# Two-layer encoder trunk: later load of x's second half, weight-sum transfers that wait, ordered splits, and a first 1/rms by GpSimd

## The chip, the cores and the metric

The kernel runs on one core of a Trainium2 chip. The metric is the device time of one execution in microseconds. Its engines are named as the profile names them: PE (TensorE, matrix products), DVE (VectorE), ACT (ScalarE), POOL (GpSimd) and SP (SyncE, which here only issues transfers). Each engine runs its own list of instructions in order; an instruction waits until those it depends on, on other engines or in transfers, are done, and holds up everything behind it in its list.

## The reference, cut to what matters

Two request groups (512 and 256 tokens, 768 in all, 1024 wide) go through two layers with shared weights, in float32. A layer is a half feed-forward, a mixer and a half feed-forward; the mixers don't matter here.

```python
def rmsnorm(x, g):
    y = x32 * lax.rsqrt(jnp.mean(x32 * x32, axis=-1, keepdims=True) + EPS)
    return y.astype(x.dtype) * g

def swiglu(h, wg, wu, wd):              # D_MODEL 1024, D_FF 2816
    return (jax.nn.silu(h @ wg) * (h @ wu)) @ wd

def even_layer(x, ...):                 # odd_layer: another mixer
    x = x + 0.5 * swiglu(rmsnorm(x, f1_n), f1_g, f1_u, f1_d)
    x = x + mixer_ab(rmsnorm(x, mix_n), ...)
    x = x + 0.5 * swiglu(rmsnorm(x, f2_n), f2_g, f2_u, f2_d)
    return x
```

## The kernel before, in words

Six phases follow one another: a feed-forward, a mixer, two feed-forwards (the second half of layer 0 and the first of layer 1), a mixer and a feed-forward. x lies transposed in eight tiles x0 to x7 (128 features by 768 tokens); its tokens are two halves of 384 columns.

Every float32 product is made of three products of rounded parts: high by high, low by high, high by low. A weight tile's high part `whi` is a cast on ACT (line 122), its low part `wlo` a subtraction on DVE (line 123). The operands made from x are split in the same way: `gain_split` (lines 404 to 410, high part on ACT at 407, low on DVE at 408) multiplies by the norm's gain, `split` (208, 209) has no gain.

A feed-forward goes through 11 pairs of weight columns, each for gate and for up. For a pair, seven products by sums of quarters replace eight (Strassen's scheme as Winograd wrote it). Their moving operands, made from x, are b11, b21, t2, t3, n4, t1 and b22; each consists of four tiles (b110 to b113). The stationary ones are quarters of the weights or sums of them: `s1` is the sum of two quarters, `s2` is `s1` and another quarter, `s3` a sum of quarters too. For most pairs DVE makes s1. For some, the early pairs among them, POOL issues a transfer that loads the first quarter into s1 and then a second that adds the other to it (`added`, line 642): a load and an accumulating load in series, for gate and for up, called weight-sum transfers here. Chain 1 makes the s1 of a feed-forward's first pair, chain 2 that of its second.

In each feed-forward the first four pairs begin early. A pair first runs two products that need neither norm nor sums, `p1` (with b11) and `p2` (with b21). `ORDERS` (line 46) mixes these steps: (0, 1, 0, 1, 2, 2, 0, 1, 3, 2, 3, 3). `p1`'s result in PSUM is copied by ACT (line 603) into a tile `p1`; `self.copied` lists those copies, two to a pair. The fifth is thus the gate's copy of the third pair. `hidden` makes the hidden units (`sg`, `v`: lines 587 to 590), which frees the PSUM banks. Later `settle` runs the other five products of a pair, first t2, which needs s2.

PE's order is as written; on the other engines and for transfers a scheduler orders instructions by priority and estimated times. `issue_after(ins)` tells it to place instructions behind `ins`; it is not a wait at run time on another engine. So before the change, the POOL queue began the first weight-sum transfers at 5.71 us, though they were placed behind a copy.

At the start, loads come on SP in the order written in `build` (from line 1684): x's first half mixed with the first four weight tiles (`first`), then x's second half, six tiles `tok` (x by tokens, for the sums of squares), and raw weight tiles of 512 KB. `second` (line 462) feeds the second half's operands, once `SECOND` copies have been scheduled. `tok_norm` (line 259) squares and sums tok on ACT, and `rsqrt` (line 314) makes 1/rms on DVE by an integer guess and three refinements (lines 317 to 328, twelve instructions on 128x3). `diags` writes it on diagonals, with which PE spreads it over the partitions.

Of the kernel before, what the change touches and what calls it, by code (L numbers as in the profile page):

```python
# [38 lines left out]
DELAYT = (0.0, 14.0), (0.0, 14.0)  # L39
TOKW, TOKQ, SECOND = (2, 8), (0, 6), 2  # L40
STEPS = (2.5, 1.5, 1.5)
# [14 lines left out]
class Trunk:  # L56
# [4 lines left out]
    def __init__(self, ctx, tc, aps, phases=PHASES):  # L61
        self.tc, self.nc, self.aps, self.phases = tc, tc.nc, aps, phases
        self.units = []
        self.woff = self.pi = 0
        self.t = 0.0
        self.chains = []
        self.spare = []
        self.first = []
        self.copied = []
        self.exps = []  # L70
# [12 lines left out]
        self.guards = {}  # L83
        self.side = "left"
# [14 lines left out]
    def raw(self, name, k0, nk, c0, n, raw=None, eng=None, **kw):  # L99
# [5 lines left out]
        if raw is None:  # L105
            raw = self.rawp.tile([P, nk * n], F32, tag="raw", name=f"raw{i}")
        (eng or self.nc.sync).dma_start(raw, src, **kw)  # L107
        if self.spare and i >= 20:
# [27 lines left out]
    def silu(self):  # L136

        self.nc.scalar.activation(self.space, self.ones[:, :96], AF.Silu)

# [119 lines left out]
    def tok_norm(self, h):  # L259
# [12 lines left out]
        with self.tc.high_priority() if h == 0 else nullcontext():  # L272
            nc.vector.tensor_tensor(out=a, in0=a, in1=b, op=ALU.add)
            self.rsqrt(y, a, 1.0 / D, a, b, it[:, :3])
            self.early[h] = self.diags(y)
# [37 lines left out]

    def rsqrt(self, y, src, scale, v, h, it):

        nc = self.nc
        nc.vector.tensor_scalar(out=v, in0=src, scalar1=scale, scalar2=EPS, op0=ALU.mult, op1=ALU.add)
        nc.vector.tensor_scalar(
# [85 lines left out]
    def gain_split(self, n, k, src, m):  # L404

        hi, lo = self.b[n][k]
        self.nc.scalar.activation(hi, src, AF.Copy, scale=self.gain(m))
        self.nc.vector.scalar_tensor_tensor(
            out=lo, in0=src, scalar=self.gain(m), in1=hi.bitcast(F32), op0=ALU.mult, op1=ALU.subtract
        )  # L410

# [50 lines left out]
    def second(self):  # L462

        while len(self.copied) < SECOND:
            yield 0.2
        with self.tc.issue_after(self.copied[SECOND - 1]):
            for m in [i // 2 + (0 if i % 2 else 4) for i in range(KD)]:
                self.feed(m, 1)
# [9 lines left out]
    def ffn(self, pre):  # L478
# [5 lines left out]
        urgent = (0, EARLY - 1) if self.first else (EARLY - 1,)  # L484
        behind = len(self.copied) + (3 if self.first else 5)
        hs = {}
# [40 lines left out]
        def pair(p):  # L527
# [24 lines left out]
            def product(n, w, b, key, start, st=None):  # L552
# [4 lines left out]
                with ExitStack() as stack:  # L557
                    if early and b in ("b11", "b21"):
                        stack.enter_context(self.tc.high_priority())
                    if early and not fresh and b in ("b11", "b21"):  # L560
                        if len(order) >= NW and order[-NW]:
# [35 lines left out]
            def p1():  # L597
                for n in names:
                    product(n, a[n, 1, 1], "b11", "X", True)
                    if early:  # L600
                        e[n, "p1"] = etile("p1")
                        with self.tc.high_priority():
                            self.copied.append(nc.scalar.copy(e[n, "p1"], bank["X", n]).ins)
                            order[-1:] = [self.copied[-1]]
                    else:
# [35 lines left out]

            def added():
                for n in names:
                    t = s[n, "s1"] = self.fw.tile([P, 4, P], F32, tag="s", name="s1", bufs=8)
                    for k, kw in ((4, {}), (0, {"accum_op": ALU.add})):
                        self.raw(f"{pre}_w_{n}", k, 4, (2 * p + 1) * P, P, t.rearrange("p a b -> p (a b)"), nc.gpsimd, **kw)
# [50 lines left out]
            if early:  # L697
                if p + 1 < EARLY - 1:
                    addeds[p + 1]()
                settle(now)  # L700
# [7 lines left out]
        for i, p in enumerate(ORDERS[mixed]):  # L708
            next(stages[p])
            if i == 8:  # L710
                with self.tc.issue_after(self.copied[behind]):
                    addeds[0]()
        for p in range(NPAIR):
# [927 lines left out]
    def build(self):  # L1641
# [17 lines left out]
        nc.gpsimd.memset(self.ones, 1.0)  # L1659
        nc.vector.tensor_copy(self.onesr, self.ones)  # L1660
        self.space = space
        self.silu()
        make_identity(nc, self.ident)
        self.gains = self.cp.tile([P, 64], F32, tag="gains", name="gains")[:, : KD * len(NORMS)]
# [19 lines left out]
        for h, (c0, c1) in enumerate(HALVES):  # L1684
            for m in range(KD):
                nc.sync.dma_start(self.x[m][:, c0:c1], self.aps["x"][m, :, c0:c1])
                if kind == "f":
                    if h == 0:
                        self.feed(m, 0)
                else:  # L1690
# [135 lines left out]
```

## Time and profile before

| | us |
|---|---|
| three runs | 2589.17, 2592.65, 2595.09 (median 2592.65) |
| the profiled execution | 2590.38, of which its span 2588.6 |
| PE busy | 2552.2 (99%) |
| DVE busy | 2232.6 (86%) |
| ACT busy | 1366.6 (53%) |
| POOL busy | 155.5 (6%) |

The mean granted clock of PE is 0.996. The times in a row of the trace are its start, in microseconds from the span's start, and its length; in brackets stand the idle time of that engine before it and what ended it. Names are those of the program without buffer numbers, and a line is often a helper's: line 152 is every product, line 122 every high part of a weight.

### The profile page before, as it was taken

To read this page: it belongs to the slowest core of one execution; us is meant where nothing else is said; L and a number is where in the kernel's file an instruction comes from. 1 tells how busy PE (TensorE), PEld (TensorE's weight loads), DVE (VectorE), ACT (ScalarE), POOL (GpSimd) and SP (SyncE) were. 2 spreads that over 40 slices of the span, in tenths; PEclk is the share of its full clock that TensorE was granted. 3 is DMA by queue.
4 is the path that set the end of the run, shared out by engine and by line. 5 is a ranking of instruction groups with operands and counts; after the bars stand their busy time and mean duration, and the time that the engine had idled before them with its cause. 6 is when DMAs were issued, how large, how long until landed. Compare 5 with 4: busy or idle time off the path is not lost.

```text
span 2588.6 us, 41317 instructions
## 1 busy us (share of the span) xinstructions
PE 2552.2 (99%) x15114; PEld 2487.2 (96%) x15114; DVE 2232.6 (86%) x4662; ACT 1366.6 (53%) x2869; POOL 155.5 (6%) x252
## 2 busy tenths in 40 slices
PE   8999999999999999999999999999999999999998
PEld 8999999988899999999999999998998999999997
DVE  7988898978879989889998889886776699888897
ACT  7544454646656545445654445454455575444543
POOL 1000000000021000000100000001222220000000
PEclk9999999999999999999999999999999999999999
DMA  7523222331144322222542222242221343222222
GB/s 246 170 81 106 72 74 74 124 100 46 58 125 132 114 66 74 74 66 98 136 109 82 66 77 71 66 145 64 64 64 41 106 134 119 82 74 74 71 66 76
DMA packets 93372, 238.68 MB, mean 92 GB/s; under 512 B 21488, under 2 KB 34288, under 8 KB 93168
## 3 DMA queue, kind: packets, MB, share of 16 engines
q1 hardware_dynamic: 85712, 218.96, 26.3%
q0 software_dynamic: 7168, 16.78, 3.1%
q8 instruction: 119, 1.95, 0.3%
q14 instruction: 85, 0.70, 0.1%
q10 hardware_dynamic: 288, 0.29, 0.0%
HBM read 226.56 MB, written 15.07 MB: 93 GB/s over the span
## 4 chain that ended last, share of the span: by engine, by line
PE 89%; DVE 6%; ACT 2%; DMA 1%; issue 1%; SPq 0%; DVEq 0%; ACTq 0%
PE ps_mm L152 54%; PE ps_aux L152 34%; PE ps_aux L156 1%; DVE wlo L123 1%; ACT p L1109 1%; DVE p L1103 1%; DMA raw<-in_w 1%; DVE tl L209 0%; DMA x<-in_x 0%; DVE tmp L415 0%; DVE p L1119 0%; ACT whi L122 0%; DVE s L739 0%; DMA first<-in_w 0%; DVE o L1254 0%
## 5 line engine op out<-in xcount | busy, mean ns | idle before, releaser
L122 ACT CAST whi<-s 128x512 fp32r<-128x512 f32 x496 | 304.6, 620 | 407.3 <-DVE s L739 177.6
L122 ACT CAST whi<-raw 128x512 fp32r<-128x512 f32 x504 | 306.1, 619 | 222.9 <-PE ps_mm L152 91.3
L123 DVE TENSOR_TENSOR wlo<-s,whi 128x512 fp32r<-128x512 f32 x496 | 336.8, 684 | 61.0 <-ACT whi L122 53.4
L123 DVE TENSOR_TENSOR wlo<-raw,whi 128x512 fp32r<-128x512 f32 x471 | 321.7, 691 | 18.2 <-ACT whi L122 14.5
L152 PE MATMUL ps_mm<-db,whi 128*128 128x384 f32 x864 | 219.2, 334 | 0.0
L152 PE MATMUL ps_aux<-dt,whi 128*128 128x384 f32 x864 | 219.2, 334 | 0.0
L152 PEld LDWEIGHTS ps_aux<-dt,whi 128*128 128x128 f32 x864 | 156.0, 188 | 0.0
L152 PEld LDWEIGHTS ps_mm<-db,whi 128*128 128x128 f32 x864 | 156.0, 188 | 0.0
L152 PE MATMUL ps_mm<-xh,whi 128*128 128x512 f32 (+1 forms) x416 | 146.2, 352 | 0.0
L152 PE MATMUL ps_aux<-dt,wlo 128*128 128x384 f32 x432 | 144.4, 334 | 1.4 <-DVE wlo L123 1.4
L152 PE MATMUL ps_mm<-db,wlo 128*128 128x384 f32 x432 | 144.3, 334 | 0.0
L152 PE MATMUL ps_mm<-xh,wlo 128*128 128x512 f32 (+1 forms) x416 | 141.3, 340 | 0.0
L152 PE MATMUL ps_mm<-xl,whi 128*128 128x512 f32 (+1 forms) x416 | 141.2, 339 | 0.0
L739 DVE TENSOR_TENSOR s<-raw,raw 128x512 f32<-128x512 f32 x124 | 84.0, 685 | 25.7 <-DMA raw<-in_w 25.5
L578 DVE TENSOR_TENSOR u<-ps_aux,u 128x384 f32<-128x384 f32 x176 | 96.9, 550 | 4.9 <-PE ps_aux L152 4.8
L152 PE MATMUL ps_aux<-dh,whi 128*128 128x384 f32 x384 | 97.5, 334 | 0.0
L795 DVE TENSOR_TENSOR x<-ps_aux,x 128x384 f32<-128x384 f32 x160 | 85.3, 551 | 14.1 <-PE ps_aux L152 13.8
L1109 ACT ACTIVATE p<-p,st 128x256 f32<-128x256 f32 (+3 forms) x144 | 68.9, 480 | 49.3 <-DVE st L1107 49.2
L573 ACT COPY u<-ps_mm 128x384 f32<-128x384 f32 x176 | 83.5, 475 | 16.5 <-PE ps_mm L152 15.9
L795 DVE TENSOR_TENSOR x<-ps_mm,x 128x384 f32<-128x384 f32 x160 | 86.1, 550 | 7.1 <-PE ps_mm L152 6.8
L107 POOL DMA_DIRECT2D s<-in_w x64 | 47.1, 781 | 702.2 <-PE ps_aux L152 387.6
L152 PEld LDWEIGHTS ps_mm<-xh,whi 128*128 128x128 f32 x416 | 79.8, 192 | 9.3 <-issue 0.9
(516 smaller groups left out, 8134.1 us busy)
## 6 DMA issues: line engine op xcount, KB each, us to landing
raw<-in_w SPq DMA_DIRECT2D x346, 512.0 KB, 3.7
s<-in_w POOLq DMA_DIRECT2D x64, 256.0 KB, 5.0
xdm<-x SPq DMA_DIRECT2D x16, 384.0 KB, 2.4
x<-in_x SPq DMA_DIRECT2D x16, 192.0 KB, 6.3
tok<-in_xt SPq DMA_DIRECT2D x12, 256.0 KB, 6.5
xold<-xdm SPq DMA_DIRECT2D x8, 384.0 KB, 3.1
x<-xdm SPq DMA_DIRECT2D x8, 384.0 KB, 4.7
out_y<-y SPq DMA_DIRECT2D x8, 384.0 KB, 2.4
```

The lines of the kernel that those rows point to most:

```text
L107: (eng or self.nc.sync).dma_start(raw, src, **kw)
L122: nc.scalar.copy(hi, src)
L123: (eng or nc.gpsimd).tensor_tensor(out=lo, in0=src, in1=hi.bitcast(F32), op=ALU.subtract)
L152: self.nc.tensor.matmul(out, lhsT=lhsT, rhs=rhs, start=start, stop=stop, **kw)
L156: self.nc.tensor.transpose(out, src, self.ident)
L573: nc.scalar.copy(e[n, out], bank[key, n])
L578: nc.vector.tensor_tensor(out=t, in0=bank[key, n], in1=t, op=ALU.add)
L739: f = lambda o, x, y, op: self.nc.vector.tensor_tensor(out=o, in0=x, in1=y, op=op)
L795: nc.vector.tensor_tensor(out=o, in0=ps, in1=o, op=ALU.add)
L1103: nc.vector.tensor_tensor_reduce(out=outs[i], in0=ps_list[i], in1=adds[i], scale=1.0, scalar=init[i], op0=ALU.add, op1=ALU.max, accum_out= ...
L1109: ins = nc.scalar.activation(outs[i], outs[i], AF.Exp, bias=nm[:, i : i + 1], accum_out=sm[:, i : i + 1])
```

## The change

Four things change in the program's text.

1. `SECOND` is 6 and no longer 2. x's second half isn't loaded by `build` any more, but by `second`, once six copies have been scheduled, and placed behind the last raw load issued so far (`self.loading`). On SP the eight transfers now stand behind the six tok tiles and the first two raw loads, and ahead of the next two raw loads.
2. `added(then)` has POOL copy one element per partition of the `then`-th p1 copy into s1 ahead of its loads. The loads overwrite it and so wait for it. Chain 1 waits for the fifth copy of its feed-forward, chain 2 for the eighth. All four feed-forwards call it.
3. The first half's b11 splits of x0 to x3 have priority and are placed one behind the other, and the b11 products' weight splits behind the last of them.
4. The first 1/rms is made by one DVE instruction and GpSimd's power to -0.5, by a constant in eight columns of `space` which the warm-up activation no longer writes.

```diff
-TOKW, TOKQ, SECOND = (2, 8), (0, 6), 2
+TOKW, TOKQ, SECOND = (2, 8), (0, 6), 6
...  raw()
-        (eng or self.nc.sync).dma_start(raw, src, **kw)
+        self.loading = (eng or self.nc.sync).dma_start(raw, src, **kw).ins
...  silu()
-        self.nc.scalar.activation(self.space, self.ones[:, :96], AF.Silu)
+        self.nc.scalar.activation(self.space[:, :88], self.ones[:, :88], AF.Silu)
...  tok_norm()
-            self.rsqrt(y, a, 1.0 / D, a, b, it[:, :3])
+            self.rsqrt(y, a, 1.0 / D, a, b, it[:, :3], h == 0)
...  rsqrt(..., power=False)
+        if power:
+            nc.vector.tensor_scalar(out=v, in0=src, scalar1=scale, scalar2=EPS, op0=ALU.mult, op1=ALU.add)
+            nc.gpsimd.tensor_tensor(out=y, in0=v, in1=self.half[:, : v.shape[1]], op=ALU.pow)
+            return
...  gain_split()
-        self.nc.scalar.activation(hi, src, AF.Copy, scale=self.gain(m))
-        self.nc.vector.scalar_tensor_tensor(
+        ins = self.nc.scalar.activation(hi, src, AF.Copy, scale=self.gain(m)).ins
+        self.fed = ins, self.nc.vector.scalar_tensor_tensor(
             out=lo, in0=src, scalar=self.gain(m), in1=hi.bitcast(F32), op0=ALU.mult, op1=ALU.subtract
-        )
+        ).ins
...  second()
+        with self.tc.issue_after(self.loading):
+            for m in range(KD):
+                self.nc.sync.dma_start(self.x[m][:, H:T], self.aps["x"][m, :, H:T])
...  ffn()
-        behind = len(self.copied) + (3 if self.first else 5)
+        behind = len(self.copied) + 4
...  product()
+                    for ins in self.fed4 if fresh and early and b == "b11" and (p or n == "up") else ():
+                        stack.enter_context(self.tc.issue_after(ins))
...  p1()
+                            self.ps1.append(e[n, "p1"])
...
-            def added():
+            def added(then=None):
                 for n in names:
                     t = s[n, "s1"] = self.fw.tile([P, 4, P], F32, tag="s", name="s1", bufs=8)
+                    if then:
+                        nc.gpsimd.tensor_copy(t[:, 0, 0:1], self.ps1[then][:, 0:1])
...
-                    addeds[p + 1]()
+                    addeds[p + 1](behind + 3 if p == 0 else None)
...
             if i == 8:
-                with self.tc.issue_after(self.copied[behind]):
-                    addeds[0]()
+                addeds[0](behind)
...  build()
+        self.half = space[:, 88:96]
+        nc.gpsimd.memset(self.half, -0.5)
...
             for m in range(KD):
-                nc.sync.dma_start(self.x[m][:, c0:c1], self.aps["x"][m, :, c0:c1])
+                if kind != "f" or h == 0:
+                    nc.sync.dma_start(self.x[m][:, c0:c1], self.aps["x"][m, :, c0:c1])
                 if kind == "f":
                     if h == 0:
-                        self.feed(m, 0)
+                        with ExitStack() as stack:
+                            if m < 4:
+                                stack.enter_context(self.tc.high_priority())
+                            for ins in self.fed if 0 < m < 4 else ():
+                                stack.enter_context(self.tc.issue_after(ins))
+                            self.feed(m, 0)
+                            self.fed4 = self.fed if m < 4 else self.fed4
```

The scheduler's estimates change with this, and so does the order on DVE and ACT at places far from the edit. PE's order stays as it was, but for the two products by the second half's diagonals, which stand one product earlier. In the order of the changed kernel the line numbers are larger by 1 at the top of the file and by 12 further down (739 is 751, 587 is 597, 603 is 613, 795 is 807).

DVE in the first feed-forward, before: where the fourth pair's first product gets its bank (`sg` and `v` from the ps_mm banks read the early pairs' first products), and the first user of a weight-sum transfer (s_716, from s_606).

```order
L123 TENSOR_TENSOR wlo_619<-raw_556,whi_618 128x512
L415 SCALAR_TENSOR_TENSOR tmp<-x_104,ngains,tmp 128x384
L209 TENSOR_TENSOR t30l<-tmp,t30h 128x384
L587 TENSOR_TENSOR sg<-ps_mm_252,acc 128x384
L589 TENSOR_TENSOR v<-ps_mm_271,acc 128x384
L587 TENSOR_TENSOR sg<-ps_mm_290,acc 128x384
L123 TENSOR_TENSOR wlo_684<-raw_558,whi_683 128x512
L739 TENSOR_TENSOR s_716<-s_606,raw_708 128x512
L589 TENSOR_TENSOR v<-ps_mm_375,acc 128x384
```

The same place after; s_592 is now the transferred sum.

```order
L751 TENSOR_TENSOR s_705<-s_592,raw_697 128x512
L210 TENSOR_TENSOR t22l<-tmp,t22h 128x384
L420 SCALAR_TENSOR_TENSOR tmp<-tmp,ngains 128x384
L420 SCALAR_TENSOR_TENSOR tmp<-x_104,ngains,tmp 128x384
L597 TENSOR_TENSOR sg<-ps_mm_245,acc 128x384
L124 TENSOR_TENSOR wlo_708<-s_705,whi_707 128x512
L599 TENSOR_TENSOR v<-ps_mm_264,acc 128x384
L597 TENSOR_TENSOR sg<-ps_mm_283,acc 128x384
L599 TENSOR_TENSOR v<-ps_mm_325,acc 128x384
```

The sum s moved from behind `sg`, `v` and `sg` to ahead of them all.

DVE near 150 us, before: the first down projection ends (it adds to the x tiles), and the five products of the fourth pair begin with t2. s_1776 is its gate's s2 and s_1782 its up's; sg, u and db belong to the pair before.

```order
L795 TENSOR_TENSOR x_108<-ps_aux_1536,x_108 128x384
L739 TENSOR_TENSOR s_1776<-s_1462,raw_1764 128x512
L795 TENSOR_TENSOR x_109<-ps_aux_1545,x_109 128x384
L123 TENSOR_TENSOR wlo_1779<-s_1776,whi_1778 128x512
L795 TENSOR_TENSOR x_110<-ps_aux_1554,x_110 128x384
L739 TENSOR_TENSOR s_1776<-raw_1764,s_1776 128x512
L209 TENSOR_TENSOR db_1805<-sg,db_1804 128x384
L497 TENSOR_TENSOR sg<-u_1248,sg 128x384
L739 TENSOR_TENSOR s_1782<-s_1467,raw_1770 128x512
L739 TENSOR_TENSOR s_1808<-raw_1764,raw_1767 128x512
```

After, where the gate's s2 is s_1770 and the up's s_1776:

```order
L807 TENSOR_TENSOR x_108<-ps_aux_1521,x_108 128x384
L807 TENSOR_TENSOR x_109<-ps_aux_1530,x_109 128x384
L807 TENSOR_TENSOR x_110<-ps_aux_1539,x_110 128x384
L751 TENSOR_TENSOR s_1776<-s_1461,raw_1764 128x512
L807 TENSOR_TENSOR x_111<-ps_aux_1548,x_111 128x384
L751 TENSOR_TENSOR s_1802<-raw_1758,raw_1761 128x512
L124 TENSOR_TENSOR wlo_1779<-s_1776,whi_1778 128x512
L751 TENSOR_TENSOR s_1776<-raw_1764,s_1776 128x512
L124 TENSOR_TENSOR wlo_1805<-s_1802,whi_1804 128x512
L210 TENSOR_TENSOR db_1799<-sg,db_1798 128x384
L751 TENSOR_TENSOR s_1825<-raw_1764,raw_1767 128x512
L505 TENSOR_TENSOR sg<-u_1242,sg 128x384
```

The up's s2 moved from behind `db` and `sg` to between the last two additions to x.

DVE near 290 us, where a down projection follows on a pair, before: v reads the pair's last product, s_3268 is a sum of two raw weight tiles for the down projection.

```order
L587 TENSOR_TENSOR sg<-ps_mm_2977,acc 128x384
L739 TENSOR_TENSOR s_3268<-raw_3258,raw_3261 128x512
L589 TENSOR_TENSOR v<-ps_mm_2996,acc 128x384
L739 TENSOR_TENSOR s_3270<-s_3268,raw_3258 128x512
L590 SCALAR_TENSOR_TENSOR sg<-sg,v 128x384
L123 TENSOR_TENSOR wlo_3277<-s_3268,whi_3276 128x512
L123 TENSOR_TENSOR wlo_3313<-raw_3252,whi_3312 128x512
```

After, where it is s_3262:

```order
L597 TENSOR_TENSOR sg<-ps_mm_2971,acc 128x384
L599 TENSOR_TENSOR v<-ps_mm_2990,acc 128x384
L600 SCALAR_TENSOR_TENSOR sg<-sg,v 128x384
L210 TENSOR_TENSOR dt_3351<-sg,dt_3350 128x384
L751 TENSOR_TENSOR s_3262<-raw_3252,raw_3255 128x512
L751 TENSOR_TENSOR s_3264<-s_3262,raw_3252 128x512
L751 TENSOR_TENSOR s_3444<-raw_3246 128x512
L124 TENSOR_TENSOR wlo_3271<-s_3262,whi_3270 128x512
```

It moved from ahead of `v` to behind `v`, `sg` and `dt`.

ACT in the fourth phase (layer 1's first feed-forward), before: s_14398 is s2 of the first pair, made from the transferred sum; the copy p_14292 is the first of the fourth pair, and p2 of that pair, which adds to the same bank ps_mm_14273, waits for it.

```order
L122 CAST whi_14366<-raw_14271 128x512
L588 ACTIVATE sg<-sg 128x384
L122 CAST whi_14400<-s_14398 128x512
L122 CAST whi_14412<-s_14410 128x512
L603 COPY p_14292<-ps_mm_14273 128x384
L595 COPY ps_mm_14416<-p_14006 128x384
L595 COPY ps_mm_14438<-p_14029 128x384
L122 CAST whi_14434<-s_14432 128x512
L603 COPY p_14334<-ps_mm_14294 128x384
```

After, where s2 has the number 14398 too and the copies are p_14290 and p_14332:

```order
L123 CAST whi_14366<-raw_14269 128x512
L123 CAST whi_14400<-s_14398 128x512
L605 COPY ps_mm_14418<-p_14004 128x384
L613 COPY p_14290<-ps_mm_14271 128x384
L605 COPY ps_mm_14440<-p_14027 128x384
L613 COPY p_14332<-ps_mm_14292 128x384
L598 ACTIVATE sg<-sg 128x384
L123 CAST whi_14414<-s_14412 128x512
```

The gate's `whi` stands ahead of that copy in both, the up's moved behind both copies. What s_14398 waits for is new: its weight-sum transfer now follows the fifth copy, p_14196, six rows above.

More of the change, by code (lines that the diff above doesn't have):

```diff
@@ L69, in __init__ @@
         self.copied = []
+        self.ps1 = []
         self.exps = []
@@ L312, in diags, with rsqrt @@
         return res
-    def rsqrt(self, y, src, scale, v, h, it):
+    def rsqrt(self, y, src, scale, v, h, it, power=False):
         nc = self.nc
+        if power:
+            nc.vector.tensor_scalar(out=v, in0=src, scalar1=scale, scalar2=EPS, op0=ALU.mult, op1=ALU.add)
+            nc.gpsimd.tensor_tensor(out=y, in0=v, in1=self.half[:, : v.shape[1]], op=ALU.pow)
+            return
         nc.vector.tensor_scalar(out=v, in0=src, scalar1=scale, scalar2=EPS, op0=ALU.mult, op1=ALU.add)
```

## The prediction

> **What bounds the kernel now.** I read the page first: the share of each engine and the chain that ended last.
>
> ```profile
> PE 2552.2 (99%) x15114; PEld 2487.2 (96%) x15114; DVE 2232.6 (86%) x4662; ACT 1366.6 (53%) x2869; POOL 155.5 (6%) x252
> PE 89%; DVE 6%; ACT 2%; DMA 1%; issue 1%; SPq 0%; DVEq 0%; ACTq 0%
> ```
>
> TensorE is the bound, and the change takes no matmul away. So only TensorE's idle time, and the time for which its clock is halved, can be won or lost. All of a gain or a loss must lie at a few stalls. Next the waits of PE from 0 to 60 us, and then windows:
>
> ```profile
> PE ps_mm L152 <- ACT p L603: 3.3, 1, 3.3
> PE ps_mm L152 <- ACT b111h L407: 1.0, 1, 1.0
> PE ps_aux L152 <- ACT diag L306: 0.7, 1, 0.7
> PE ps_aux L152 <- DVE diag L308: 0.3, 1, 0.3
> ```
>
> ```profile
> 20.00:30.00 10.00, 6.65 (x31) 6.33 (x30) 5.59 (x13) 8.57 (x23) 0.00 (x0) 0.85 1.04 394
> 40.00:50.00 10.00, 10.00 (x59) 10.00 (x58) 9.75 (x19) 10.00 (x26) 2.91 (x4) 1.00 0.84 211
> 150.00:160.00 10.00, 6.87 (x30) 6.52 (x31) 7.72 (x13) 4.90 (x10) 0.00 (x0) 0.83 0.41 117
> ```
>
> The columns are the window, its length, busy time and count of PE, PEld, DVE, ACT and POOL, the granted clock, the DMA share and GB/s. Two stretches run at a lowered clock, 0.85 and 0.83: each follows a stall of over 3 us. From 40 us DVE and ACT are full, so a lead of TensorE can be kept there only as far as ACT and DVE follow. The timeline gives the places of the first block:
>
> ```profile
> 21.04 1.12 ACT L395 ACTIVATE tmp<-x,gains 128x384 f32<-128x384 f32 x2 [3.28 <-DMA x<-in_x]
> ...
> 26.86 0.61 PE L152 MATMUL ps_mm<-b210h,whi 128*128 128x384 f32 x1 [3.35 <-ACT p L603]
> 27.27 0.52 PE L152 MATMUL ps_mm<-b210l,whi 128*128 128x384 f32 x1
> 27.59 0.52 PE L152 MATMUL ps_mm<-b210h,wlo 128*128 128x384 f32 x1
> ...
> 32.72 0.33 PE L152 MATMUL ps_aux<-b110h,whi 128*128 128x384 f32 x1
> 32.89 0.33 PE L152 MATMUL ps_aux<-b110l,whi 128*128 128x384 f32 x1
> ...
> 42.93 0.33 PE L152 MATMUL ps_mm<-b110h,whi 128*128 128x384 f32 x1
> ...
> 34.99 0.48 ACT L603 COPY p<-ps_aux 128x384 f32<-128x384 f32 x1 [1.59 <-PE ps_aux L152]
> ```
>
> ACT stood 3.28 us in front of a tmp that wanted x's second half; two p copies queued behind it, and TensorE waited 3.35 us for them. Afterwards its matmuls stand 0.32 us apart (27.27 to 27.59) instead of 0.17 (32.72 to 32.89). The copy at 34.99 is the fifth of a p1; 42.93 is the first product of the early stage's fourth pair.
>
> **The change, part by part.** (1) The lead in the first block. x's second half goes behind six tok tiles and two raw loads: 2.5 MB, at 394 GB/s 6.4 us. The two weight-sum chains that ran there leave, 1 MB or 2.7 us. A piece that arrived at 21.04 so comes at about 24.7, the last by some 26. ACT's first tmp of it now stands behind the fifth copy (27.6, below), so this delay is covered; without that cover TensorE would wait for p again. The waits that go: 3.3 (p), 1.0 (b111h; the ordered splits), 1.0 for the two diag (0.7 + 0.3, as 1/rms comes earlier), and the lowered clock, 0.15 of 10 us, 1.5 us of work. The first stretch runs cold; without the b111h stall I expect full clock one interval of about 3.4 us earlier, which at half speed is 1.6 us (an estimate, from the length of the slow stretch that starts at 26.86; it could be 0). Sum 8.4 us. TensorE is then at the fourth pair at 42.93 - 8.4 = 34.5, and the fifth copy (ahead of the diag waits) at 34.99 - 7.4 = 27.6.
>
> (2) The new wait takes it back. The POOL copy lets the weight-sum transfers go only after that fifth copy: 27.6 + 0.48, and two tiny copies. Their price isn't in the trace, so it is bounded by the rows at hand: from nothing to GpSimd's 0.79 us below; I take 0.15 each, as they move one element per partition. Then a load and an accumulating load follow in series:
>
> ```profile
> 41.30 0.57 POOL L107 DMA_DIRECT2D s<-in_w  x1 [27.36 <-ACT tok L271]
> 42.89 0.56 POOL L107 DMA_DIRECT2D s<-in_w  x1 [1.02 <-ACT tok L271]
> 44.51 0.90 POOL L107 DMA_DIRECT2D s<-in_w  x1 [1.06 <-DMA s<-in_w]
> 47.19 0.88 POOL L107 DMA_DIRECT2D s<-in_w  x1 [1.78 <-DMA s<-in_w]
> ...
> DMA to landing us min/median/max: 2.9/5.1/7.1
> ```
>
> The third and fourth start when the first and second have landed: 3.2 and 4.3 us. For the accumulate I take the median to the longest of these eight, 5.1 to 7.1. So gate's sum lands 8.3 to 11.4 us after its issue, at 36.7 to 39.8. Behind it on DVE stands, in order, the sum s (0.68 us), then three instructions and the sg that frees the bank of the fourth pair's first product: 2.9 us in all, so 39.6 to 42.7 instead of 42.93, 3.3 to 0.2 us better. TensorE idles 5 to 8 us there, longer than the 3.35 that cost it its clock, so 1.5 us go again: 1.8 us better to 1.3 worse. Between these I take 0.3 better: nearer the late end, because the first transfer starts while tok and raw loads fill the queue, and DVE's work of those 5 to 8 us is queued behind s with ACT and DVE full from 40 on. The Trainium skill ("DMA: Bandwidth & Descriptors", "Anatomy of one DMA — SWDGE (gpsimd) path") gives about 2.0 us and size over 436 GB/s for such a transfer, 2.6 us for 256 KB. By that estimate the chain would be 5.2 us and this term 3.5 us better; the rows here, 3.2 and 4.3 us for the lighter load alone, disagree.
>
> (3) The power. It replaces twelve DVE instructions of about 0.16 us by one DVE and one GpSimd instruction on 128x3. No power is in the trace; the nearest rows of GpSimd are:
>
> ```profile
> 4.96 0.79 POOL L1667 TENSOR_SCALAR ngains<-gains 128x56 f32<-128x56 f32 x1 [3.50 <-DMA gains<-in_gains]
> 697.89 1.40 POOL L123 TENSOR_TENSOR wlo<-raw,whi 128x512 fp32r<-128x512 f32 x1 [586.56 <-DVE p L1119]
> ```
>
> So nothing to 1.4 us; I take 0.8, nearest in size. tok now travels ahead of the third pair's raw, and TensorE wants that pair at 32.72 - 7.4 = 25.3; ahead of it two casts and two wlo must run (some 2.5 us), which stand behind diag on ACT and yh on DVE. So 1/rms may come as late as some 22 us, while the squares, with tok there some 2.5 us before the raw loads, should end near 20 (an estimate): cost 0, and only what lasts over about 2 us delays the third pair.
>
> (4) The hand-over from the first down projection to the fourth pair's t2. The changed times move DVE's order here, and this is the largest term.
>
> ```profile
> 149.75 0.51 ACT L208 CAST db<-sg 128x384 fp32r<-128x384 f32 x1
> 150.29 0.56 DVE L209 TENSOR_TENSOR db<-sg,db 128x384 fp32r<-128x384 f32 x1 [1.97 <-ACT db L208]
> 150.89 0.56 DVE L497 TENSOR_TENSOR sg<-u,sg 128x384 f32<-128x384 f32 x1
> 151.36 0.68 DVE L739 TENSOR_TENSOR s<-s,raw 128x512 f32<-128x512 f32 x1
> 152.14 1.22 ACT L122 CAST whi<-s 128x512 fp32r<-128x512 f32 x2 [1.88 <-DVE s L739]
> 152.81 0.45 PE L152 MATMUL ps_mm<-t20h,whi 128*128 128x384 f32 x1 [3.47 <-ACT whi L122]
> ```
>
> DVE waits for db and sg, which ACT and TensorE's gate product hold back, before it makes the up's s2: TensorE stands 3.47 us. In the changed order this s is two rows ahead of both, among the x additions. The stall goes, and with it the lowered clock (0.17 of 10 us, 1.7): 5.2 us, of which I leave 0.7 (one cast and the wlo behind it) as what is late next: -4.5. Bounds: -5.2, and 0 if another wait ends there too.
>
> (5) The opposite, at the step to down projections near 290 us:
>
> ```profile
> 288.68 0.68 DVE L739 TENSOR_TENSOR s<-raw,raw 128x512 f32<-128x512 f32 x1
> 290.28 0.56 DVE L589 TENSOR_TENSOR v<-ps_mm,acc 128x384 f32<-128x384 f32 x1 [0.92 <-PE ps_mm L152]
> 291.82 0.68 DVE L123 TENSOR_TENSOR wlo<-s,whi 128x512 fp32r<-128x512 f32 x1
> 289.63 0.62 ACT L122 CAST whi<-s 128x512 fp32r<-128x512 f32 x1
> 292.56 0.45 PE L152 MATMUL ps_aux<-dt,wlo 128*128 128x384 f32 x1 [1.45 <-DVE wlo L123]
> ```
>
> Now s stands ahead of v; then it stands behind v, sg and dt: v at 290.28, three steps of 0.6 to 292.0, then s, a second s and a copy (3 x 0.6) to 293.8 and wlo to 294.5. TensorE's wlo product starts at 294.5 instead of 292.56: +1.9.
>
> (6) The later feed-forwards get the same wait (there the loads left early). Rows of the fifth copy and of the first user, in the third and the fourth phase:
>
> ```profile
> 783.78 0.46 ACT L603 COPY p<-ps_mm 128x384 f32<-128x384 f32 x1
> 794.47 0.68 DVE L739 TENSOR_TENSOR s<-s,raw 128x512 f32<-128x512 f32 x1
> 1271.69 0.48 ACT L603 COPY p<-ps_aux 128x384 f32<-128x384 f32 x1 [1.59 <-PE ps_aux L152]
> 1282.56 0.33 PE L152 MATMUL ps_mm<-b210h,whi 128*128 128x384 f32 x1
> ```
>
> Third: 783.78 + 0.46 + 0.3 + 8.3 to 11.4 is 792.8 to 795.9, against 794.47: 0 to +1.4, I take +0.6; the last phase runs the same code and is taken as the same, +0.6. Fourth: 1272.5 + 8.3 to 11.4 is 1280.8 to 1283.9. There ACT has whi of this s ahead of the copy that the product at 1282.56 waits for, so s 0.68, whi 0.62, two copies (0.95) and their hand-overs follow, 2.6 us: 1283.4 to 1286.5, +0.8 to +3.9. I take +2.0.
>
> **Sum:** -0.3 + 0 - 4.5 + 1.9 + 0.6 + 0.6 + 2.0 = +0.3. The profiled execution took 2590.38 us (span 2588.6), so 2590.7 by its own time; it lies 2.3 under the median of the runs, 2592.65, so I predict 2593.0.
>
> **Rivals.** Slow chains (slower): every chain takes the 11.4 us end. Then +1.3, +1.4, +1.4 and +3.9, the fourth phase's stall is over 3 us and costs 1.5 of clock, +1.9 and -4.5 stay: +6.9, 2599.5. It decides from a chain of about 10.5 us. For it: the longest row, 7.1, and loads that compete with raw; against it: the quick 3.2.
>
> Quick chains (faster): gate's and up's chain in about 6 us (twice the shortest landing, 2.9). Then (2) is held only by ACT, full from 40 to 50: some 3.5 us better (its p copies of the fourth pair then come some 3.5 us sooner); (6) is 0: -3.5 - 4.5 + 1.9 = -6.1, 2586.5. Against it: the median landing, 5.1.
>
> The hand-over stalls elsewhere: (4) gives 0, since what feeds it is one chain of small hand-overs: +4.8, 2597.5.
>
> A slow power: some 4 us over its cover delays the third pair and the fourth copy of the chain: +4 on the sum, 2597.0. The Trainium skill ("GPSIMD Engine Reference", "2.1 Instruction dispatch") tells of about 6 us at the first call of a newly loaded kernel; whether power needs one no run here shows, and the first TENSOR_TENSOR at 697.89 took 1.40.
>
> **Chances.** Forecast 0.45, slow chains 0.22, quick chains 0.17, hand-over 0.09, power 0.07. Within 0.2% (5.2 us, about what a measurement of this kernel can tell from no change) lie the forecast nearly whole, a part of each chain case and the nearer half of the last two: same 0.55. Faster 0.20: quick chains for the most part and 0.07 of the forecast's end. Slower 0.25: slow chains and the far half of hand-over and power. Range 2585.5 to 2600.5: both chain cases with a margin of one us.
>
> **What would show it.** Right: the 3.35 us wait for p gone; one new idle of 5 to 8 us before the fourth pair, ended through DVE by the weight-sum transfer; no 3.47 us at 150 and no lowered clock there; a wait of 3 to 4 us near 290; 1 to 4 us in the fourth phase. Wrong: sums that land under 7 us or over 12 us after their issue, GpSimd's power over 2 us, or the lowered clock at other places than these.

## The result and the profile after

The changed kernel takes 2606.84 us (median of six runs, 2599.15 to 2608.60), the kernel before 2592.43 (six runs beside it). The ratio is 1.0056, with a 95% interval of 1.0046 to 1.0066: slower by 0.56%, some 14.4 us. The forecast was 2593.0, with a range up to 2600.5. The profiled execution after took 2607.18 us (span 2605.4), 16.8 more than the one before.

First the page's shares of the engines and the chain that ended last, after:

```profile
PE 2557.6 (98%) x15114; PEld 2493.9 (96%) x15114; DVE 2231.2 (86%) x4650; ACT 1366.0 (52%) x2869; POOL 163.0 (6%) x270
PE 84%; DVE 9%; DMA 3%; ACT 2%; issue 2%; POOL 0%; DVEq 0%; ACTq 0%; SPq 0%; POOLq 0%
```

PE runs the same 15114 products. Its share of the chain falls from 89% to 84%, DVE's and DMA's rise: products wait for sums that wait for transfers. The waits of PE after, in the windows 0 to 60, 170 to 300, 700 to 900, 1230 to 1320 and 2080 to 2180 us (what it waited for: total, times, longest), show where:

```profile
PE ps_mm L153 <- DVE sg L597: 9.6, 1, 9.6
...
PE ps_aux L153 <- ACT whi L123: 2.8, 1, 2.8
PE ps_aux L153 <- DVE wlo L124: 0.5, 1, 0.5
...
PE ps_mm L153 <- DVE wlo L124: 2.6, 2, 2.0
...
PE ps_mm L153 <- ACT p L613: 4.0, 1, 4.0
...
PE ps_mm L153 <- DVE wlo L124: 1.8, 1, 1.8
PE ps_mm L153 <- ACT whi L123: 1.0, 2, 0.7
```

From 100 to 170 us there is none: the 3.47 us of the hand-over are gone, and so are the waits for p, b111h and the diag tiles in the first block. Waits at five places stand instead: before the fourth pair (9.6), at the step to down projections (2.8 and 0.5), and in the three later feed-forwards (2.6, 4.0, 2.8).

Since PE's order is the same, the same product can be compared. This table gives when it starts in a kernel, less when it starts before (us, from the traces; the columns are the times before):

| kernel | 33 | 121 | 231 | 337 | 619 | 964 | 1345 | 2037 | 2210 | end |
|---|---|---|---|---|---|---|---|---|---|---|
| after | -8.3 | +1.8 | -4.4 | +0.5 | +3.2 | +4.7 | +11.3 | +11.5 | +16.8 | +16.8 |
| e1_no_wait | -6.8 | +1.8 | -4.5 | -1.0 | -1.4 | -1.4 | -1.5 | -1.4 | -0.3 | -0.3 |
| e2_wait_first | -7.8 | +2.4 | -3.9 | -0.2 | +4.1 | +3.9 | +4.0 | +4.2 | +5.0 | +5.3 |
| e3_only_waits | -3.6 | -1.1 | -0.1 | -0.1 | +4.2 | +6.9 | +13.2 | +13.4 | +17.7 | +18.0 |
| e4_early_copy | -7.4 | +0.3 | -6.0 | -2.6 | -3.0 | -2.9 | +2.8 | +3.0 | +5.6 | +5.6 |
| e7_before_wait_first | -3.9 | -1.4 | -0.5 | -0.5 | -0.9 | -2.0 | -2.0 | -2.0 | -0.5 | -0.5 |
| e8_feed_later | -8.6 | +3.0 | -3.3 | -3.3 | -0.6 | -1.0 | -1.1 | -1.1 | +1.1 | +1.1 |
| e9_no_power | -8.5 | +3.9 | -2.4 | -2.4 | +0.4 | +0.5 | +0.5 | +0.4 | +3.7 | +3.7 |
| e10_splits_before | -4.2 | +8.1 | +1.8 | +1.8 | +1.4 | +0.5 | +0.5 | +0.5 | +1.3 | +1.3 |
| e11_third_copy | -6.1 | +0.8 | -5.5 | -5.5 | -2.7 | -3.3 | -3.4 | -3.4 | -1.5 | -1.5 |
| e12_no_wait_later_feed | -7.5 | +0.1 | -6.2 | -6.2 | -1.9 | -1.3 | -1.4 | -1.4 | -0.4 | -0.4 |
| e13_wait_fourth | -8.1 | -0.5 | -6.8 | -2.1 | +0.6 | -0.9 | +5.0 | +5.0 | +5.3 | +5.3 |
| e14_again | -9.0 | +1.3 | -5.0 | -0.4 | +2.3 | +6.2 | +12.9 | +13.1 | +17.8 | +17.8 |

The first block ends at 121, the hand-over lies between 121 and 231, the step near 290 before 337, the first mixer before 619, the third phase before 964, the fourth before 1345, and the last begins near 2037. Read along the first row: PE is 8.3 us ahead in the first block and gives it all back before 121; it gains 6.2 at the hand-over, loses 4.9 at the step near 290, 2.7 in the first mixer, 1.5 in the third phase, 6.6 in the fourth and 5.3 in the last.

The chain of waits from 20 to 50 us, after, in order of time (start, length, what), tells the first return:

```profile
26.65 0.49 ACT p L613
...
27.19 0.32 POOL s L657 x2
...
27.69 6.22 DMA s<-in_w
...
34.21 1.98 DMA s<-in_w
36.19 0.47 DVE tmp L398
36.66 3.37 issue
40.03 0.20 DVE s L751
...
40.64 0.55 DVE t22l L210
41.19 1.06 DVE tmp L420 x2
42.25 0.48 DVE sg L597
...
42.77 7.32 PE ps_mm L153 x29
```

The fifth copy ends, POOL touches both s1 tiles, the load takes 6.22 us, and the accumulating load goes out at 34.21. DVE then stands 3.37 us until s at 40.03, 12.3 us after the first issue. The view names no releaser for it (issue), but the accumulating load of 34.21 took 5.7 us to land, so it landed just ahead of s. Four DVE instructions later sg frees the bank, and PE goes on at 42.77. The fourth phase, the chain from 1270 to 1295:

```profile
1276.42 0.49 ACT p L613
...
1276.96 0.98 POOL s L657 x2
1277.94 2.84 DMA s<-in_w
...
1281.15 0.94 DMA s<-in_w
1282.09 0.47 DVE sg L600
1282.56 6.62 issue
1289.18 0.70 DVE s L751
```

Here the load took 2.84 us, and from the accumulating load's issue at 1281.15 to s at 1289.18 it is 8.0; this load took 7.9 us to land. Before, no wait stood here; the loads left 38 us earlier, as a row of POOL in the timeline before shows:

```profile
1239.90 1.12 POOL L107 DMA_DIRECT2D s<-in_w  x2 [384.59 <-PE ps_aux L152]
```

Last the windows after (columns as in the prediction; the last four numbers are POOL, granted clock, DMA share and GB/s): at each of the new waits, at the hand-over (150) and in the first mixer (600):

```profile
40.00:50.00 10.00, 7.23 (x30) 7.23 (x31) 9.80 (x21) 8.58 (x20) 0.20 (x1) 0.64 0.19 27
150.00:160.00 10.00, 10.00 (x60) 10.00 (x59) 9.93 (x19) 7.85 (x17) 0.00 (x0) 1.00 0.77 213
290.00:300.00 10.00, 9.68 (x40) 9.68 (x41) 7.63 (x15) 3.82 (x9) 0.00 (x0) 0.68 0.17 52
600.00:610.00 10.00, 10.00 (x45) 8.19 (x44) 6.77 (x23) 2.23 (x8) 0.00 (x0) 0.66 0.23 65
800.00:810.00 10.00, 7.55 (x42) 6.76 (x40) 9.48 (x28) 4.84 (x10) 1.77 (x2) 1.00 0.39 74
1290.00:1300.00 10.00, 8.56 (x36) 8.56 (x37) 8.23 (x24) 6.37 (x13) 3.23 (x6) 0.68 0.40 91
2130.00:2140.00 10.00, 7.48 (x33) 6.84 (x32) 8.28 (x24) 3.72 (x7) 1.77 (x2) 0.83 0.62 128
```

The clock is whole at 150, where it was 0.83, and lowered at five places. At 0.68 a busy window of 10 us loses 3.2 us of work, which is near the length of the waits ahead of it.

### The profile page after: what moved, and what is told of

The parts are those of the page before. It is cut to its first block, busy times and chain, and to the rows that moved or that the text cites. A ratio compares the mean times of both kernels' runs of the same rounds, so it can differ in the third digit from the quotient of the medians.

```text
span 2605.4 us, 41321 instructions
## 1 busy us (share of the span) xinstructions
PE 2557.6 (98%) x15114; PEld 2493.9 (96%) x15114; DVE 2231.2 (86%) x4650; ACT 1366.0 (52%) x2869; POOL 163.0 (6%) x270
## 4 chain that ended last, share of the span: by engine, by line
PE 84%; DVE 9%; DMA 3%; ACT 2%; issue 2%; POOL 0%; DVEq 0%; ACTq 0%; SPq 0%; POOLq 0%
PE ps_mm L153 52%; PE ps_aux L153 32%; DVE wlo L124 2%; DMA s<-in_w 1%; DMA raw<-in_w 1%; PE ps_aux L157 1%; DVE s L751 1%; ACT p L1121 1%; DVE p L1115 1%; DVE tl L210 0%; DVE p L1131 0%; DVE u L588 0%; DVE o L1266 0%; ACT whi L123 0%; PE ps_aux L1697 0%
## 5 line engine op out<-in xcount | busy, mean ns | idle before, releaser
L751 DVE TENSOR_TENSOR s<-s,raw 128x512 f32<-128x512 f32 x124 | 84.9, 684 | 19.6 <-issue 15.4
L807 DVE TENSOR_TENSOR x<-ps_aux,x 128x384 f32<-128x384 f32 x160 | 85.3, 551 | 13.5 <-PE ps_aux L153 13.4
L124 POOL TENSOR_TENSOR wlo<-raw,whi 128x512 fp32r<-128x512 f32 x33 | 43.4, 1321 | 731.2 <-DVE p L1131 587.7
```

Of the source, the lines that this page charges most:

```text
L124: (eng or nc.gpsimd).tensor_tensor(out=lo, in0=src, in1=hi.bitcast(F32), op=ALU.subtract)
L751: f = lambda o, x, y, op: self.nc.vector.tensor_tensor(out=o, in0=x, in1=y, op=op)
L807: nc.vector.tensor_tensor(out=o, in0=ps, in1=o, op=ALU.add)
```

## The experiments

No kernel here changes what is computed. The first theory (A) was that the loss lies in the later feed-forwards, whose transfers now leave late. The rivals put it in the first block or in the changed order of DVE.

**e1_no_wait**: the changed kernel without POOL's copies.

```diff
-                    if then:
+                    if False:
```

> The changed kernel with POOL's copies left out, so that no weight-sum transfer waits; x's order, the splits' order and the power stay, and DVE's order at 150 and 290 us is that of the changed kernel. Theory A (the waits cost it): the 9.6 us wait before the fourth pair goes, so do the 4.0 us in the fourth phase, the 1.8 + 1.0 in the last and the 2.0 in the third, each with its lowered clock. Against the kernel before the rest is then a lead of 2 to 3.5 us in the first block, -6 at 150, +5 at 290: 2588 us, 2583 to 2594. Theory B (the waits are harmless; x's order, the power or DVE's new order, with lowered clock at 290 and in the mixer, cost it): 2602 or more.

Measured: 2592.96 us, ratio 1.0006 [0.9997, 1.0016]. The waits of the later phases are gone and the table's row stays flat from 337 on. But the wait before the fourth pair stays, at 7.6 us (waits of PE, 0 to 60):

```profile
PE ps_mm L153 <- DVE sg L597: 7.6, 1, 7.6
```

So in the first block the new wait isn't needed for a stall. (DVE and ACT run in another order here than in the changed kernel from 22 to 53 us, since the scheduler's estimates differ.) The chain of e1 from 20 to 45 us begins with transfers of x and raw, beside which the weight-sum transfers run again; then comes DVE's own work, without idle time before s:

```profile
15.30 10.35 DMA x<-in_x
...
25.71 4.76 DMA raw<-in_w
...
39.34 0.47 DVE tmp L398
39.81 0.07 DVE s L751
...
41.94 0.48 DVE sg L597
```

**e2_wait_first**: copies only in the first feed-forward.

```diff
-                    if then:
+                    if then and pre == "l0_ffn1":
```

> The changed kernel with the waits in the first feed-forward only; the first 1300 us of the order are alike. Theory A: the three later feed-forwards lose nothing any more, which is 2.5 + 6.5 + 4.8 us by the drift of matmuls between the two traces: 2593 us, 2589 to 2598, with the 9.6 us wait and its lowered clock still there. Theory B: 2602 or more.

Measured: 2592.66, ratio 1.0007 [0.9998, 1.0015]. By the ratios, the waits of the three later feed-forwards cost 0.49%, 12.7 us, of the 14.4. The first one's wait costs nothing that can be told from e1. In the third and the last phase DVE and ACT run in the same order in both kernels, so the waits alone differ. In the fourth phase their order from 1274 to 1306 us changes together with the wait.

**e3_only_waits**: the kernel before with the copies alone (edit 2), waiting for the same copies.

> The kernel before, with the waits alone (copies by POOL, same copies of p1 as in the change); x, splits and 1/rms as before, and DVE's order at 150 and 290 us as before. Theory A: the later feed-forwards lose the same 13 to 14 us; in the first block the fifth copy comes at 35, the sum lands near 47, ahead of t2 at 51, so that little is lost there, 0 to 4: 2608 us, 2602 to 2613. Theory B: 2592 to 2598.

Measured: 2606.87, ratio 1.0061 [1.0049, 1.0074], the whole of the change's loss without its other parts. Behind 320 us its DVE and ACT run in the order of the changed kernel, the fourth phase's new order included; there no run parts order and wait. In the first block it is even 1.1 us ahead at 121 us, since x and raw come earlier; the stalls at 150 (3.5) and 290 (1.4) are those of before, so edit 2 doesn't move them. Its wait in the fourth phase (waits of PE, 1230 to 1320) is that of the changed kernel:

```profile
PE ps_mm L153 <- ACT p L604: 4.2, 1, 4.2
```

**e4_early_copy**: chain 1 waits for the second copy, chain 2 for the fifth.

```diff
-                    addeds[p + 1](behind + 3 if p == 0 else None)
+                    addeds[p + 1](behind if p == 0 else None)
...
-                addeds[0](behind)
+                addeds[0](behind - 3)
```

> The changed kernel with the waits on earlier copies: chain 1 on the second p1 copy of its feed-forward instead of the fifth, chain 2 on the fifth instead of the eighth. Theory A, which says that it is the landing and not the wait as such: chain 1 is issued near 17 us in the first block and lands by 30, before DVE comes to its sum, and some 12 us earlier in the later ones: no stall, about 2587 us, 2582 to 2593. Theory B: 2602 or more.

Measured: 2595.84, ratio 1.0016 [1.0007, 1.0024]: most of the loss is gone, though not all that was expected. DVE and ACT run in e1's order from end to end, so between e1 and this run only the copies and the times of the transfers differ. What is lost in the table are 5.7 us in the fourth phase and 2.6 in the last. In the fourth, chain 2, now on the fifth copy, sends its accumulating loads at 1273.55 and 1274.33, and the slower of them takes 11.1 us. A raw load sent between them lands only at 1283.2, and DVE stands for it:

```profile
1283.21 0.69 DVE L751 TENSOR_TENSOR s<-raw,raw 128x512 f32<-128x512 f32 x1 [3.71 <-DMA raw<-in_w]
```

In e1 the same step stood 0.68 us. PE waits 2.5 us a little later. That chain 2's loads hold up the raw load is argued from these times, not shown.

**e13_wait_fourth**: copies in the fourth phase alone (`pre == "l1_ffn1"`), to price the waits of one phase.

> The changed kernel with the waits in the fourth phase only (layer 1's first feed-forward). The run without any wait took 2593.0 us; in the changed kernel's trace 4.0 us of waiting and a lowered clock put the matmuls 6.5 us back in this phase. If that is the price of this wait alone: 2599.5 us, 2597 to 2602. If it only shows where lateness from elsewhere comes out: 2593 to 2595.

Measured: 2595.79, ratio 1.0026 [1.0014, 1.0037], against e1's 1.0006: 0.20%, some 5 us by the ratios and 2.8 by the medians, for one wait of 3.6 us and a clock of 0.66 after it. That lies between the two expectations; in the table this phase takes 5.9 us, near the changed kernel's 6.6. The window of it from 1280 us:

```profile
1280.00:1290.00 10.00, 6.39 (x27) 6.07 (x26) 4.92 (x13) 3.34 (x7) 1.45 (x4) 0.66 0.39 117
```

**e7_before_wait_first**: e3 with e2's limit, so the kernel before with the wait in the first feed-forward alone.

> The kernel before with the waits in the first feed-forward only, nothing else. In the run of the waits alone that feed-forward ended 1.2 us ahead of before, since x and raw no longer share the queue with 1 MB of weight-sum transfers, and the 3.35 us wait for p fell to 0.7. If that is all: 2590 us, 2587 to 2593, same or up to 0.15% faster. If the waits hurt in the first block too: 2594 or more.

Measured: 2592.39, ratio 1.0012 [1.0003, 1.0021]. The profiled run is 1.4 us ahead at 121, yet by the ratio the kernel is slower by 0.12%: the small gain doesn't last. Against e3 the three later phases' waits cost 0.49% here too, as between e2 and the changed kernel.

**e8_feed_later**: from here on the question was whether the 8 us of lead can be kept. e2, with the operands of x's second half placed behind the first hidden units and, at the step near 290, s2 ahead of v.

```diff
-        with self.tc.issue_after(self.copied[SECOND - 1]):
+        while not self.hids:
+            yield 0.2
+        with self.tc.issue_after(self.hids[0]):
...  down()
-        s2 = sums("s2")
+        with self.tc.high_priority() if pre == "l0_ffn1" and pairs[0] == 4 else nullcontext():
+            s2 = sums("s2")
```

> The changed kernel with the waits in the first feed-forward only, and x's second-half operands made on DVE and ACT behind the first pair's hidden units: sg stands ahead of t2's tmp and of the sum s, and at 290 us s comes to stand ahead of v again. Theory C (the stall before the fourth pair is DVE's order: sg behind seventeen instructions of x's second half; without any wait it was still 7.6 us): that stall falls to 2 us or less, the first block is 3 to 5 us ahead of the run that differs in this alone, 290 us gives 3.7 more: 2584 us, 2580 to 2588. Theory D (late transfers decide there, by whatever order): the stall stays at 6 us or more, only 290 gives: 2588 to 2592.

Measured: 2591.49, ratio 1.0003 [0.9995, 1.0012]: not the gain hoped for. The fourth pair's p1 no longer waits, but its p2 does, for a copy by ACT, 10.4 us. Waits of PE, then pieces of the chain from 20 to 50 us:

```profile
PE ps_mm L153 <- ACT p L615: 10.4, 1, 10.4
```

```profile
27.41 7.03 DMA s<-in_w
...
36.19 4.32 issue
40.51 0.70 DVE s L753
...
47.08 0.37 ACT p L615
```

DVE stands 4.32 us for the sum, and then ACT makes operands for 6 us before the copy that PE needs. The wait at 290 is back to 1.4 and that step costs 0 in the table, where e2 lost 3.7: the order of s and v is what cost it. In e8 and the runs built on it, DVE's order at 290 us is that of the kernel before.

**e9_no_power**: e8 with the first 1/rms by DVE, as before.

```diff
-            self.rsqrt(y, a, 1.0 / D, a, b, it[:, :3], h == 0)
+            self.rsqrt(y, a, 1.0 / D, a, b, it[:, :3])
```

> The run with the later feed, but with 1/rms by DVE's twelve instructions as before. If GpSimd's power saves a wait for diag in the first block (0.7 + 0.3 before the change): 1 to 2 us slower than the run with it. If it is off the path: the same within 2 us. DVE's order at 290 us is that with s ahead of v in both.

Measured: 2590.13, ratio 1.0002 [0.9994, 1.0011]: the same as e8.

**e10_splits_before**: e8 without edit 3 (the splits in the scheduler's own order).

> The run with the later feed, but with the first half's splits placed as before (no priority, not one behind the other). If the ordered splits bring the 1.0 us wait for b111h and the earlier full clock (1.6): the fourth product group of the first block starts 2 to 3 us later than in the run with them; if that lead is taken up by DVE and ACT, full from 40 us, the whole time is the same within 1.5 us, else 2 to 3 us slower.

Measured: 2599.02, ratio 1.0036 [1.0024, 1.0048], 0.33% slower than e8, some 8.6 us and far more than either expectation. The wait for b111h is back (waits of PE, 0 to 60), the lead at 33 us halves from 8.6 to 4.2, and the stall before the fourth pair is 11.3 us:

```profile
PE ps_mm L153 <- ACT b111h L412: 1.6, 1, 1.6
```

So here the ordered splits are worth their place. Its profiled run, 2591.73, was the quickest of its six, so the table's end understates this loss, and where the rest of the 8.6 us arises no trace shows.

**e11_third_copy**: e8, chain 1 on the third copy (`addeds[0](behind - 2)`).

> The run with the later feed, but chain 1 of the first feed-forward waits for the third p1 copy (near 17 us) instead of the fifth (near 26). In the run with the later feed DVE still stood 4.3 us for that sum, and ACT's whi 4.0 behind it. If that wait is what is left of the first block's stall: the sum lands near 29, x's second half some 2 us later, the stall before p2 of the fourth pair falls from 10.4 us to 6 or less, and the whole is 3 to 5 us ahead of the run with the later feed: 2587 us, 2583 to 2590. If DVE and ACT set the end there by the amount of their work for x's second half (rival): the stall stays at 8 us or more and the time within 2 us of that run.

Measured: 2588.84, ratio 0.9997 [0.9988, 1.0006], 2.7 us under e8 by the medians, between the two expectations; the intervals overlap. DVE no longer waits for the sum; PE still waits 6.2 us for the same copy by ACT. It also waits 2.2 us at 26.96 for a `wlo` behind the first 1/rms, since the power now stands on POOL behind the two accumulating loads (its row starts at 24.45 instead of 20.29).

**e12_no_wait_later_feed**: e8 without any wait for chain 1 (`addeds[0](behind - 4)`).

> The run with the later feed, with chain 1 not waiting at all (its loads start near 6 us and share the queue with x and the first weights). If late x and raw loads cost what the missing wait saves, as between the two runs of the changed order (2593.0 without and 2592.7 with the first wait): within 2 us of the run with the later feed, 2591.5. If the wait on DVE is what is left: 3 to 5 us faster.

Measured: 2588.15, ratio 0.9991 [0.9982, 1.0000], 3.3 us under e8 by the medians, though the intervals touch; the quickest kernel of all, but not told apart from the one before. It still waits 7.1 us, and its chain from 20 to 50 us has no weight-sum transfer in it, but raw loads and ACT's work, the squares of the second half's tok among it:

```profile
14.68 9.36 DMA raw<-in_w
...
25.83 4.54 DMA raw<-in_w
...
34.31 1.22 ACT tok L272 x4
...
44.94 0.37 ACT p L615
```

**e14_again**: the changed kernel once more, one profile.

> The changed kernel unaltered, profiled once more. If the places of the lowered clock belong to the program (near 43, 291, 1292 and 2135 us, and 601 us in the first mixer), all come again. If the last hangs on where a stall meets the clock's own period, which differs from run to run: those behind the long stalls come again, 601 may be elsewhere or missing.

Measured: 2608.28. The waits at the five places come again (10.3; 2.8 and 0.2; 3.2 and 0.6; 3.9; 2.6), and so does the loss in the first mixer. The lowered clock comes at the same five places and at one more, in the third phase.

## Why the prediction was wrong, step by step

**Step (6), the later feed-forwards, failed.** Its mechanism was right and its size was not: +3.2 us forecast (0.6, 2.0 and 0.6), 13.4 measured in the trace (1.5, 6.6, 5.3). The experiments bear it out from both sides: without these waits 12.7 us come back (e2), and the waits alone cost as much as the whole change (e3). In the fourth phase, half of it, the new order on DVE and ACT came with the wait, so that part rests on the trace: DVE stands until the load lands. Three prices in the step were too low.

- The accumulating load was put at 5.1 to 7.1 us by the landings from 40 to 80 us before. In the fourth phase it took 7.9, and in the first block the plain load, put at 3.2 to 4.3, took 6.2. First issue to s was 12.3 us in the first block and 11.2 in the fourth phase, where 8.3 to 11.4 was forecast and about the middle taken. Over 12 us was the prediction's own sign of being wrong. The Trainium skill ("DMA: Bandwidth & Descriptors", "Anatomy of one DMA — SWDGE (gpsimd) path") makes 2.6 us of one such transfer, an estimate by its fit. The fourth phase's plain load, 2.84, comes near it; the first block's 6.22 and the accumulating load's 7.9 do not, and the measurement decides.
- POOL's two copies were put at 0.3 together. In the fourth phase they took 0.98.
- Of the new stalls, the clock was priced only for the one before the fourth pair. The fourth phase's waits of 4.0 us were followed by a clock of 0.68, up to 3.2 us of work in 10; the last phase's 2.8 by 0.83, 1.7. That the last phase would repeat the third was wrong for this reason: waits of 2.6 and 2.8 us (1.3 and 2.3 more than before) cost 1.5 where the clock stayed whole and 5.3 where it did not. Of these 5.3, the waits and the clock explain 4, and a wait of PE for `u` near 2197 us, 1.1 where it was 0.2, another 0.9.

The trace before already held longer landings, outside the window that the prediction read. These two rows are for its weight-sum transfers from 0 to 25 and from 780 to 800 us:

```profile
DMA to landing us min/median/max: 6.1/6.6/7.9
...
DMA to landing us min/median/max: 3.0/4.7/9.2
```

From first issue to last landing, gate's and up's sum took 13.3 and 14.4 us in the first of these windows.

The rival "slow chains" named this mechanism and stood at 2599.5, still 7.3 us under the measured median: of the later phases it priced the clock in one only, and it put no clock on the step near 290 and nothing on the mixer.

**Step (1)** held: 8.4 us of lead forecast, 8.3 seen at 33 us, and the waits that it named are gone. e10 shows that about half of it is the ordered splits.

**Step (2)** held in kind: the lead goes into one idle before the fourth pair. It was 9.6 us instead of 5 to 8, and the block ended at +1.8 instead of -0.3, a term 2.1 us too low. Its reason was only half right. Without the wait the stall is still 7.6 (e1), and when DVE's queue is rearranged, it becomes a wait for ACT (e8, e12). What refuses the lead is read from the chains of e1 and e12: work on DVE and ACT for the second half and for raw weights, from loads that end between 24 and 30.5 us. That is argued, since no kernel took this work away. Late transfers add 2 to 4 us to it (9.6 against 7.6 in e1; e8's 10.4, with DVE standing for the sum, against 7.1 in e12 and 6.2 in e11). No kernel here had more than 1.4 us left of the lead at 121 us.

**Step (3)** held: power took 0.90 us against 0.8 forecast, and e9 shows no difference without it. The Trainium skill's 6 us for a first call ("GPSIMD Engine Reference", "2.1 Instruction dispatch") did not appear: this row of POOL is short, and it starts 0.16 us after DVE's `sm` has ended:

```profile
20.29 0.90 POOL L320 TENSOR_TENSOR sm<-sm,space 128x3 f32<-128x3 f32 x1 [14.57 <-DVE sm L319]
```

**Step (4)** held and was a little better, -6.2 for -4.5: stall and lowered clock both went.

**Step (5)** had the right place and the right wait: 3.3 us instead of 1.4 is the +1.9 forecast. It cost 4.9, since the clock fell to 0.68 behind it, and no clock was in that term. e2 and e8 show that the order of s and v makes it. With the same waits, e1, e2 and e4 lose 3.4 to 3.7 us here; their clock is at half for 3.4 us and not for 6.8.

**Not forecast:** +2.7 in the first mixer, where no instruction was touched. The prediction read two stretches of lowered clock before, each behind a stall of over 3 us. The trace before holds two more, both in this mixer, and no wait ahead of them is over 1.5 us. One of the two is this window:

```profile
583.40:586.80 3.40, 3.40 (x16) 2.96 (x15) 2.85 (x10) 2.85 (x6) 0.00 (x0) 0.50 0.00 0
```

After, it is gone; PE then waits 1.7 us for DVE's `o` near 596, where it waited 0.6, and the clock is at half from 600.1 for 6.8 us. A lowered clock at a place that the prediction didn't name was one of its signs of being wrong. The late stretch comes in most of the variants and not in e1, e4, e7 and e10. The first three of these have the early one instead, and a wait of 0.2 us for `o`. Why the early one goes is open. The measured parts sum to +1.8 - 6.2 + 4.9 + 2.7 + 1.5 + 6.6 + 5.3 = 16.6 (and 0.2 between the fourth phase and the last), against 16.8 in the profiled executions and about 14.4 in the medians.

## What to carry to other kernels

A prefetch that is only placed late still starts early; turning that into a wait at run time delays it in every block that shares the code, so price the chain end to end in each of them, with the slowest landings in the trace rather than the middle ones. Look for landings in the whole trace and not in one quiet window. Add the clock to every new stall of about 2 us or more, as a chance at least: here a fall cost up to 1.7 us of work for each 3.4 us at half. And where an engine's lead ends at work that other engines must do anyway, removing one wait may only change the name of the next, as in e8 and e12.

## What the hardware showed beyond expectation

The lowered clock needs no single long wait. In the last phase the longest wait was 1.8 us and the clock fell to 0.83, while in the third phase, with a longest of 2.0 and nearly the same idle time in the window (7.48 and 7.55 of 10 us busy), it stayed at 1.00. In e14 the third phase fell to 0.83 too, there behind a wait of 3.2. Taken by itself, the last phase's stretch runs at half:

```profile
2136.10:2139.50 3.40, 3.40 (x13) 3.40 (x12) 3.40 (x11) 1.58 (x3) 0.00 (x0) 0.50 0.84 128
```

The end of each trace aside, the stretches at half last 3.4 us or two, three or four times as long. The Trainium skill ("TensorE: Matmul & The Clock Gate", "Part 1") tells of a free-running window of about 3.4 us, so that the moment of a change varies, and gives an idle window of that length as what lowers the clock. The lengths of the stretches agree with such a window; an idle time of 3.4 us as the condition does not, since 1.8 was enough here.

POOL's two copies of one element per partition took 0.30 us in the first block, but 1.15 in the third and 1.04 in the fourth phase (0.98 up to the first load), 0.32 for the fourth phase's second chain and 2.03 for the third phase's. What makes the difference wasn't tried.
